# Moving the last loaded piece of a row-sum kernel to byte 64 of its buffer, with new bounds for the last two rows' pieces

## The chip, the cores and the metric

The kernel runs on one core of one Trainium2 chip. The metric is the device time of one execution in microseconds (us). A profiled execution has in addition a span, from its first to its last recorded instruction, some 1.35 us shorter than the time.

## The reference

```python
batch, seq, dim = 32, 512, 1024          # x: float32
relu_x = np.maximum(x, 0)
return np.sum(relu_x, axis=-1).astype(np.float32)
```

16,384 rows of 1024 floats are clipped at zero and summed: 67.1 MB in, 65 KB out.

## The kernel before

Each of the 128 partitions takes 128 rows. SyncE issues all loads: large chunks of 16 rows, then 8, 4 and 2 rows, and at last two rows cut by columns into four pieces. VectorE and ScalarE clip and sum. The last two rows matter here. Seen as one run of 2048 columns, they are cut so that the last transfer, the seam, holds the end of the first row and the head of the second in one small buffer of its own. Beside the seam's columns stand the partial sums of the other pieces, so that one instruction per row finishes both.

```python
CUT = 912
HEAD = 256
    ...
    w = D - CUT
    seam = nc.alloc_sbuf_tensor("seam", [P, 2 + w + HEAD + 2], fp32)
    ...
    first, second, third = [(0, CUT), (D + D // 2, 2 * D), (D + HEAD, D + D // 2)]
    for k, (lo, hi) in enumerate((first, second, third)):
        sp.dma_start(out=flat[:, lo:hi], in_=rows[:, lo:hi]).then_inc(...)
    sp.dma_start(out=seam[:, 2 : 2 + w + HEAD], in_=rows[:, CUT : D + HEAD]).then_inc(s_seam, 16)
    ...
    # first: half on each engine; second: ScalarE; third: VectorE
    act.wait_ge(s_seam, 16 + 2)
    act.wait_ge(s_half, 2)
    on_act(seam[:, 0:k], res[:, J - 2 : J - 1]).then_inc(s_last, 1)      # row 1: k = 2 + w
    dve.wait_ge(s_seam, 16 + 2)
    on_dve(seam[:, k : k + HEAD + 2], res[:, J - 1 : J]).then_inc(s_last, 1)   # row 2
```

The wait on `s_seam` counts 16 from the seam's transfer, one from ScalarE when the second piece is summed, and one from VectorE for the third. I call the moment at which it is full the **release**, and that at which a transfer's 16 counts are full its **landing**.

Of the kernel before, what the change touches and what calls it, by code (L numbers as in the profile page):

```python
# [3 lines left out]
P = 128  # L4
D = 1024
# [4 lines left out]
ACT_STEPS = [[16], [7, 9], [7, 9], [7, 9], [4, 5, 7], [3, 4, 5]]  # L10
DVE_STEPS = [[4, 5, 7], [7, 4, 5], [7, 4, 5], [7, 4, 5], [4, 5, 7], [3, 4, 5]]
TAIL = [8, 4, 2]
CUT = 912
HEAD = 256


def bass_relu_sum_kernel(
# [14 lines left out]
    fp32 = mybir.dt.float32  # L32
# [5 lines left out]
    J = B * S // P  # L38
# [11 lines left out]

    buf = nc.alloc_sbuf_tensor("buf", [P, NB, BIG, D], fp32)
    w = D - CUT
    seam = nc.alloc_sbuf_tensor("seam", [P, 2 + w + HEAD + 2], fp32)
    res = nc.alloc_sbuf_tensor("res", [P, J], fp32)
    turned = nc.alloc_sbuf_tensor("turned", [P, 32], fp32)

# [6 lines left out]
    s_half = nc.alloc_semaphore("s_half")  # L63
    s_seam = nc.alloc_semaphore("s_seam")
    s_last = nc.alloc_semaphore("s_last")
# [4 lines left out]
    sp, act, dve = nc.sync, nc.scalar, nc.vector  # L70
# [14 lines left out]
    for c in range(NBIG + 1):  # L85
        if c >= NB:
            sp.wait_ge(s_dve, done[c - NB])
        if c < NBIG:
            i = 0
            for g, j, n in CHUNKS[c]:  # L90
                sp.dma_start(  # L91
                    out=buf[:, c % NB, i : i + n, :], in_=xv[g][:, j : j + n, :]
# [14 lines left out]

    rows = xv[-1].rearrange("p j d -> p (j d)")[:, r * D : (r + 2) * D]
    flat = buf[:, tb, r : r + 2, :].rearrange("p j d -> p (j d)")
    first, second, third = [(0, CUT), (D + D // 2, 2 * D), (D + HEAD, D + D // 2)]  # L110
    for k, (lo, hi) in enumerate((first, second, third)):
        sp.dma_start(out=flat[:, lo:hi], in_=rows[:, lo:hi]).then_inc(  # L112
            s_in[NBIG + len(TAIL) + k], 16
        )
    sp.dma_start(out=seam[:, 2 : 2 + w + HEAD], in_=rows[:, CUT : D + HEAD]).then_inc(s_seam, 16)
    sp.wait_ge(s_turn, 1)
    sp.dma_start(
        out=of[0:P].rearrange("(k q) -> k q", q=32), in_=turned[0:P:32, 0:32]
# [7 lines left out]
    def on_act(t, acc):  # L126
        return act.activation(t, t, AF.Relu, accum_out=acc)  # L127

    def on_dve(t, acc):
        return dve.tensor_scalar(  # L130
            out=t, in0=t, scalar1=0.0, scalar2=None, op0=ALU.max, op1=ALU.add, accum_out=acc
        )
# [4 lines left out]
    k = 0  # L137
    for c in range(NTWO):
# [17 lines left out]
        for n in DVE_STEPS[c]:  # L156
            if ready[r + n - 1] > seen:
# [3 lines left out]
                out=res[:, c * BIG + r : c * BIG + r + n],  # L161
                in_=buf[:, c % NB, r : r + n, :],
# [24 lines left out]
    lo, hi = first  # L187
    act.wait_ge(s_in[-3], 16)
    dve.wait_ge(s_in[-3], 16)
    on_act(flat[:, lo : CUT // 2], seam[:, 0:1]).then_inc(s_half, 1)  # L190
    on_dve(flat[:, CUT // 2 : hi], seam[:, 1:2]).then_inc(s_half, 1)
    k = 2 + w
    lo, hi = second
    act.wait_ge(s_in[-2], 16)
    on_act(flat[:, lo:hi], seam[:, k + HEAD : k + HEAD + 1]).then_inc(s_seam, 1)
    lo, hi = third
    dve.wait_ge(s_in[-1], 16)
    on_dve(flat[:, lo:hi], seam[:, k + HEAD + 1 : k + HEAD + 2]).then_inc(s_seam, 1)
    act.wait_ge(s_seam, 16 + 2)
    act.wait_ge(s_half, 2)  # L200
    on_act(seam[:, 0:k], res[:, J - 2 : J - 1]).then_inc(s_last, 1)
    dve.wait_ge(s_seam, 16 + 2)
    on_dve(seam[:, k : k + HEAD + 2], res[:, J - 1 : J]).then_inc(s_last, 1)

# [33 lines left out]
```

## Time and profile before

| | before |
|---|---|
| time, median of 3 runs | 160.86 us (160.75 to 160.93) |
| span | 159.4 us |
| VectorE, ScalarE busy | 76%, 64% |
| load queue: time of its packets, as a share of the span of 16 DMA engines | 98.1% |
| HBM read and written over the span | 421 GB/s |
| release to issue of the last store | 0.48 us |

The chain of waits is to be read from its end: the last store, the two seam instructions, what released them. Where several events release one wait, the chain names one of them, so others that came within a few ns of it don't appear. Those are in the trace's records of semaphore updates, which I use beside the chain and which decide the order. A **packet** is one record of one DMA engine; each of the last four pieces is 128 packets, one for each partition, 8 on each engine.

### The profile page before, as it was taken

What the parts mean: (1) busy time and instruction counts of PE and PEld (TensorE: products, weight loads), DVE (VectorE), ACT (ScalarE), POOL (GpSimd) and SP (SyncE); (2) the same over time, 40 slices, a digit from 0 to 9 for tenths busy, and PEclk for the clock granted to TensorE, in tenths of its full rate; (3) what the DMA queues carried; (4) which work ended last, traced back from release to release, by engine and by line L of the source; (5) the groups of instructions that cost most, each with busy time, mean ns of one, the idle gap of its engine ahead of it and who ended that gap; (6) DMA issues with size and microseconds to landing.
All of it is one profiled execution on the core that took longest, in us unless ns stands there. A gap on an engine that the chain in (4) does not pass through costs nothing.

```text
span 159.4 us, 150 instructions
## 1 busy us (share of the span) xinstructions
DVE 120.6 (76%) x59; ACT 101.5 (64%) x54; POOL 0.2 (0%) x4
## 2 busy tenths in 40 slices
DVE  0000000009999999999999999999999999898995
ACT  3000059980799708996099941999329980496975
POOL 0000000000000000000000000000000000000000
DMA  9997996996996997989979969969969979798994
GB/s 378 493 401 339 493 526 263 526 526 263 526 493 296 526 444 345 526 378 411 526 312 477 526 263 526 526 263 526 526 263 526 444 345 526 321 469 374 417 400 142
DMA packets 2457, 67.18 MB, mean 421 GB/s; under 512 B 536, under 2 KB 792, under 8 KB 1176
## 3 DMA queue, kind: packets, MB, share of 16 engines
q1 hardware_dynamic: 2456, 67.18, 98.1%
q14 instruction: 1, 0.01, 0.0%
HBM read 67.11 MB, written 0.07 MB: 421 GB/s over the span
## 4 chain that ended last, share of the span: by engine, by line
DVE 55%; DMA 34%; ACT 9%; SPq 2%; issue 0%
DVE res L160 54%; DMA buf<-in_x_dram 34%; ACT buf L145 9%; SPq L101 1%; SPq L112 1%; DVE buf L130 0%; DVE seam L130 0%; SPq L91 0%; DVE turned L169 0%
## 5 line engine op out<-in xcount | busy, mean ns | idle before, releaser
L160 DVE TENSOR_REDUCE res<-buf 128x4 f32<-128x4096 f32 (+3 forms) x18 | 99.4, 5596 | 35.5 <-ACT buf L145 35.5
L145 ACT ACTIVATE buf<-buf 128x7168 f32<-128x7168 f32 (+5 forms) x13 | 80.4, 6233 | 46.1 <-DMA buf<-in_x_dram 46.1
L127 ACT ACTIVATE buf<-buf 128x1024 f32<-128x1024 f32 (+2 forms) x19 | 19.0, 999 | 8.9 <-DMA buf<-in_x_dram 8.9
L130 DVE TENSOR_SCALAR_CACHE_REDUCE buf<-buf 128x1024 f32<-128x1024 f32 (+2 forms) x19 | 20.7, 1143 | 1.7 <-DMA buf<-in_x_dram 1.6
L127 ACT ACTIVATION_READ_ACCUMULATOR buf<-buf 128x1 f32 x19 | 3.6, 188 | 0.0
L145 ACT ACT_TABLE_LOAD x1 | 1.3, 1283 | 1.3 <-PEq L223 1.3
L130 DVE DVE_READ_ACCUMULATOR buf<-buf 128x1 f32 x19 | 1.6, 84 | 0.0
L130 DVE TENSOR_SCALAR_CACHE_REDUCE seam<-seam 128x258 f32<-128x258 f32 x1 | 0.4, 421 | 0.0
L127 ACT ACTIVATE seam<-seam 128x114 f32<-128x114 f32 x1 | 0.3, 300 | 0.1
L169 DVE STREAM_TRANSPOSE turned<-res 128x32 f32<-128x32 f32 x1 | 0.2, 211 | 0.0
L127 ACT ACTIVATION_READ_ACCUMULATOR seam<-seam 128x1 f32 x1 | 0.2, 186 | 0.0
L223 POOL MEMSET const-bfloat16-1.0<- 128x1 bf16 x1 | 0.1, 101 | 0.0
L223 POOL MEMSET const-uint8-127<- 128x1 uint8 x1 | 0.1, 101 | 0.0
L223 POOL MEMSET const-float32-0.0<- 128x1 f32 x1 | 0.1, 98 | 0.2 <-issue 0.2
L223 POOL MEMSET const-float32-1.0<- 128x1 f32 x1 | 0.1, 98 | 0.0
L130 DVE DVE_READ_ACCUMULATOR seam<-seam 128x1 f32 x1 | 0.1, 82 | 0.0
## 6 DMA issues: line engine op xcount, KB each, us to landing
buf<-in_x_dram SPq DMA_DIRECT2D x1, 7680.0 KB, 21.1
buf<-in_x_dram SPq DMA_DIRECT2D x1, 4096.0 KB, 25.3
buf<-in_x_dram SPq DMA_DIRECT2D x1, 2048.0 KB, 29.9
buf<-in_x_dram SPq DMA_DIRECT2D x1, 1024.0 KB, 31.9
buf<-in_x_dram SPq DMA_DIRECT2D x1, 512.0 KB, 3.3
buf<-in_x_dram SPq DMA_DIRECT2D x1, 456.0 KB, 32.5
buf<-in_x_dram SPq DMA_DIRECT2D x1, 256.0 KB, 32.7
seam<-in_x_dram SPq DMA_DIRECT2D x1, 184.0 KB, 32.6
```

The costliest lines, as they stand in the source:

```text
L101: sp.dma_start(out=buf[:, tb, r : r + n, :], in_=xv[-1][:, r : r + n, :]).then_inc(s_in[NBIG + i], 16)
L112: sp.dma_start(out=flat[:, lo:hi], in_=rows[:, lo:hi]).then_inc(s_in[NBIG + len(TAIL) + k], 16)
L127: return act.activation(t, t, AF.Relu, accum_out=acc)
L130: return dve.tensor_scalar(out=t, in0=t, scalar1=0.0, scalar2=None, op0=ALU.max, op1=ALU.add, accum_out=acc)
L145: act.activation(t, t, AF.Relu).then_inc(s_act, 1)
L160: dve.tensor_reduce(out=res[:, c * BIG + r : c * BIG + r + n], in_=buf[:, c % NB, r : r + n, :], axis=X, op=ALU.add,).then_inc(s_dve, 1)
L169: dve.transpose(out=turned[:, :], in_=res[:, 0:32]).then_inc(s_turn, 1)
L223: nc = _bacc.Bacc("TRN2", target_bir_lowering=False, num_devices=1)
```

## The change

The intent: the seam's columns start 64 bytes into their buffer instead of 8, with the two partial sums of the first row just ahead of them. The bounds of the pieces move so that the seam also starts at a multiple of 256 bytes in memory, and the work is dealt anew between the engines.

```diff
-CUT = 912
-HEAD = 256
+CUT = 896
+HEAD = 240
+MID = 464
@@
+    z = 16
-    seam = nc.alloc_sbuf_tensor("seam", [P, 2 + w + HEAD + 2], fp32)
+    seam = nc.alloc_sbuf_tensor("seam", [P, z + w + HEAD + 2], fp32)
@@
-    first, second, third = [(0, CUT), (D + D // 2, 2 * D), (D + HEAD, D + D // 2)]
+    first, second, third = [(0, CUT), (D + MID, 2 * D), (D + HEAD, D + MID)]
@@
-    sp.dma_start(out=seam[:, 2 : 2 + w + HEAD], in_=rows[:, CUT : D + HEAD])...
+    sp.dma_start(out=seam[:, z : z + w + HEAD], in_=rows[:, CUT : D + HEAD])...
@@
-    on_act(flat[:, lo : CUT // 2], seam[:, 0:1])...
-    on_dve(flat[:, CUT // 2 : hi], seam[:, 1:2])...
-    k = 2 + w
+    on_act(flat[:, lo : CUT // 2], seam[:, z - 2 : z - 1])...
+    on_dve(flat[:, CUT // 2 : hi], seam[:, z - 1 : z])...
+    k = z + w
@@
-    on_act(seam[:, 0:k], res[:, J - 2 : J - 1])...
+    on_act(seam[:, z - 2 : k], res[:, J - 2 : J - 1])...
```

In columns: first piece 912 to 896, second 512 to 560, third 256 to 224, seam 368 before and after.

More of the change, by code (lines that the diff above doesn't have):

```diff
@@ L114, in bass_relu_sum_kernel @@
         )
-    sp.dma_start(out=seam[:, 2 : 2 + w + HEAD], in_=rows[:, CUT : D + HEAD]).then_inc(s_seam, 16)
+    sp.dma_start(out=seam[:, z : z + w + HEAD], in_=rows[:, CUT : D + HEAD]).then_inc(s_seam, 16)
     sp.wait_ge(s_turn, 1)
@@ L189, in bass_relu_sum_kernel @@
     dve.wait_ge(s_in[-3], 16)
-    on_act(flat[:, lo : CUT // 2], seam[:, 0:1]).then_inc(s_half, 1)
-    on_dve(flat[:, CUT // 2 : hi], seam[:, 1:2]).then_inc(s_half, 1)
-    k = 2 + w
+    on_act(flat[:, lo : CUT // 2], seam[:, z - 2 : z - 1]).then_inc(s_half, 1)
+    on_dve(flat[:, CUT // 2 : hi], seam[:, z - 1 : z]).then_inc(s_half, 1)
+    k = z + w
     lo, hi = second
@@ L200, in bass_relu_sum_kernel @@
     act.wait_ge(s_half, 2)
-    on_act(seam[:, 0:k], res[:, J - 2 : J - 1]).then_inc(s_last, 1)
+    on_act(seam[:, z - 2 : k], res[:, J - 2 : J - 1]).then_inc(s_last, 1)
     dve.wait_ge(s_seam, 16 + 2)
```

## The prediction

> **What bounds the kernel now.** I read the page first, for the load of the DMA engines, then the chain of waits in order of time, then the timeline of the last microseconds, then the groups by shape. The page:
>
> ```profile
> span 159.4 us, 150 instructions
> ...
> DMA  9997996996996997989979969969969979798994
> ...
> q1 hardware_dynamic: 2456, 67.18, 98.1%
> ```
>
> The one load queue keeps the 16 DMA engines busy 98.1% of the span; VectorE (76%) and ScalarE (64%) have slack. The kernel is a 67 MB load with a short tail, and the bytes are the same after the change. So only the tail can move. The end of the chain in order of time (start, length, what):
>
> ```profile
> 124.39 32.60 DMA buf<-in_x_dram
> 156.99 0.02 issue
> 157.01 0.44 DVE buf L130 x2
> 157.45 0.02 issue
> 157.47 0.43 DVE seam L130 x2
> ```
>
> The third piece lands at 156.99, VectorE reduces it until 157.45, both engines then do their share of the seam piece, and the last store follows (issue to landing 1.4, so the span closes at 159.4). The timeline of the tail (start, length, engine):
>
> ```profile
> 155.96 0.58 ACT L127 ACTIVATE buf<-buf 128x456 f32<-128x456 f32 x1
> 156.65 0.63 ACT L127 ACTIVATE buf<-buf 128x512 f32<-128x512 f32 x1
> 157.01 0.42 DVE L130 TENSOR_SCALAR_CACHE_REDUCE buf<-buf 128x256 f32<-128x256 f32 x1 [0.40 <-DMA buf<-in_x_dram]
> 157.19 0.19 ACT L127 ACTIVATION_READ_ACCUMULATOR buf<-buf 128x1 f32 x1
> 157.36 0.08 DVE L130 DVE_READ_ACCUMULATOR buf<-buf 128x1 f32 x1
> 157.47 0.30 ACT L127 ACTIVATE seam<-seam 128x114 f32<-128x114 f32 x1
> ```
>
> And the issues with their landing times:
>
> ```profile
> buf<-in_x_dram SPq DMA_DIRECT2D x1, 256.0 KB, 32.7
> seam<-in_x_dram SPq DMA_DIRECT2D x1, 184.0 KB, 32.6
> buf<-in_x_dram SPq DMA_DIRECT2D x1, 128.0 KB, 32.6
> ```
>
> Three arrivals release the seam's arithmetic: VectorE with the third piece (157.36 + 0.08 = 157.44, its semaphore at 157.451 in the semaphore records), the seam's own landing (issued 124.87, + 32.6; 157.438 in the records), and ScalarE with the second piece (157.19 + 0.19 = 157.38). They are 13 ns and 70 ns apart. That tie is the core of what follows: **no one of the three can be worth more than its lead over the next.**
>
> [...] the seam's last packet ends at 156.967 and its semaphore fills at 157.438, 0.47 later; this doesn't depend on where the piece lands, I take it.
> [...] Pieces of 3648, 2048 and 1024 bytes take 142, 84 and 46 ns at the median with little scatter (for 1024: 46 to 51). The line through 1024 and 3648 (0.0366 ns per byte, 8.5 ns fixed) gives 62.4 ns for 1472 bytes. The seam's 128 packets take 62 at the least (52 of them), 66 at the median, 67.5 at the mean, up to 82: the one piece at byte 8 is the one with a wide scatter.
>
> **The change part by part.**
> *Seam aligned, same size.* Destination at byte 64, and its source at 896 x 4 = 3584 = 14 x 256, also aligned. 128 packets over 16 engines are 8 an engine; each loses 67.5 - 62.4 = 5 ns, so 40 ns, and perhaps 60 in the engines that end last, whose packets are the slow ones. The seam lands at about 157.39.
> *Third piece, 256 to 224 columns.* First, second and third together hold 912 + 512 + 256 = 1680 columns before and 896 + 560 + 224 = 1680 after, so the third lands when it did, 156.99. VectorE's instruction gets shorter. The groups by shape (the last columns: busy us, mean ns | idle):
>
> ```profile
> L130 DVE TENSOR_SCALAR_CACHE_REDUCE buf<-buf 128x1024 f32<-128x1024 f32 x17 | 19.8, 1217 | 1.3 <-DMA buf<-in_x_dram 1.2
> L127 ACT ACTIVATE buf<-buf 128x1024 f32<-128x1024 f32 x17 | 17.7, 1045 | 8.9 <-DMA buf<-in_x_dram 8.9
> L127 ACT ACTIVATE buf<-buf 128x512 f32<-128x512 f32 x1 | 0.6, 630 | 0.0
> L130 DVE TENSOR_SCALAR_CACHE_REDUCE buf<-buf 128x256 f32<-128x256 f32 x1 | 0.4, 420 | 0.4 <-DMA buf<-in_x_dram 0.4
> ```
>
> VectorE: (1217 - 420) / 768 = 1.04 ns per column, so 32 columns are 33 ns, and VectorE's arrival moves from 157.451 to 157.418. ScalarE: (1045 - 630) / 512 = 0.81 ns per column.
> *First piece, 912 to 896.* Its halves go from 456 to 448 columns, and it lands 64 B x 8 packets x 0.037 = 19 ns earlier: off the path, since ScalarE waits for the second piece next.
> *Second piece, 512 to 560.* First and second together grow by 32 columns = 128 B: 128 x 8 x 0.037 = 38 ns later, so it lands at 156.626 + 0.038 = 156.664. ScalarE could start at 156.648 before (just free, 22 ns after the landing); now it starts at 156.664 + 0.022 = 156.686. Its instruction grows by 48 x 0.81 = 39 ns. Its arrival was 157.380; it becomes 157.380 + 0.038 + 0.039 = **157.457**.
> *The seam's arithmetic.* VectorE 258 to 242 columns, 16 x 1.04 = 17 ns less; it is the later one now (its semaphore at 157.915, ScalarE's at 157.873), so 17 ns on the path. ScalarE 114 to 130, 16 x 0.81 = 13 ns more, to 157.886 against VectorE's 157.898 at an unmoved release: still the earlier by 12 ns.
> *Sum.* Release max(157.39 seam, 157.418 VectorE, 157.457 ScalarE) = 157.457, against 157.451: +6. Then -17. Net **-11 ns**, in 160.86 us. Instruction counts and the order on each engine are unchanged[...].
>
> **Rivals.**
> *ScalarE is not delayed.* If the second piece's landing does not follow its bytes [...], ScalarE starts at 156.648, arrives at 157.419, ties with VectorE, and the release is 32 earlier: -32 - 17 = -49 ns, 160.81. For it: the steps between landings vary (0.37 for the 1024-byte piece against 0.48 for the seam at the mean). Against: those pieces' landings keep the order and roughly the spacing of their bytes.
> *Misaligned sources eat it.* The second piece now starts 64 B and the third 192 B above a 256 B boundary. [...] Against: the seam's source starts 64 B above a boundary today, yet 52 of its packets keep to the line of the aligned ones.
> *The seam's alignment is worth far more.* If landing at byte 8 cost the whole queue something [...], the pieces before it would also come earlier. The 3648, 2048 and 1024 packets sit on one line, so I see no room above 0.1 us.
> *Verdict-size effects.* For 2% the change must move 3.2 us, more than the whole tail from the third landing to the end (159.4 - 157.0 = 2.4). Nothing in it reaches that.
>
> **Range and chances.** The mean of the three ways, weighted to the first two, is -0.01 to -0.03: 160.84. The spread of the three runs of before is 0.18, larger than all three outcomes together; the session of another measurement may shift by as much. So 160.60 to 161.05. Faster by over 2%: 0.005; slower: 0.005; within: 0.99.
>
> **What would show it.** The seam's packets at a median near 62 ns with little scatter; the third landing unmoved at 156.99 (beside the same issue times); ScalarE's 560-column instruction near 669 ns and starting some 40 ns later; VectorE's 224 and 242 columns near 387 and 404 ns; the seam's arithmetic released by ScalarE, where the chain of waits now shows VectorE's third piece. Wrong if the seam's packets keep their scatter (alignment is then not its cause), if packets of the third piece rise above the line (8.5 + 0.0366 x 896 = 41 ns), or if the time moves by more than 0.25 us, which would mean that something before the tail changed.

The sum of the forecast: +6 ns at the release and 17 ns less after it, so -11 ns, or 160.85. The three ways together, weighted to the first two, came to -10 to -30 ns, hence 160.84. The way summed above (-11 ns) and "ScalarE is not delayed" (-49 ns, 160.81) keep their terms. The third, "Misaligned sources eat it", was weighed as a loss. That aligning the seam would pay was my estimate from the packets alone, 67.5 ns at the mean against 62.4 by the line.

## The result

| | before | after |
|---|---|---|
| time, median of 6 runs | 160.90 us (160.75 to 161.02) | 160.87 us (160.81 to 160.98) |
| ratio | | 1.000 (95% interval 0.9987 to 1.0013) |

A ratio is the mean time of one kernel's fast runs over that of the other's of the same rounds, so it isn't quite the ratio of the medians quoted. The profile page of the changed kernel:

```profile
span 159.5 us, 150 instructions
...
q1 hardware_dynamic: 2456, 67.18, 98.1%
```

The load is what it was. The end of its chain of waits in order of time (start, length, what):

```profile
123.97 32.82 DMA buf<-in_x_dram
156.79 0.02 issue
156.81 0.03 ACT buf L130
156.84 0.55 issue
157.39 0.20 ACT buf L130
157.58 0.02 issue
157.61 0.41 DVE seam L133 x2
```

The releaser has changed hands. Before, the chain ran through the third piece and VectorE. Now it runs through the second piece, landing at 156.79, and ScalarE's instruction on it. (The "issue" of 0.55 is the body of that instruction, whose two records the chain splits.) The timeline of the same stretch:

```profile
156.81 0.67 ACT L130 ACTIVATE buf<-buf 128x560 f32<-128x560 f32 x1
157.11 0.39 DVE L133 TENSOR_SCALAR_CACHE_REDUCE buf<-buf 128x224 f32<-128x224 f32 x1 [0.42 <-DMA buf<-in_x_dram]
157.39 0.19 ACT L130 ACTIVATION_READ_ACCUMULATOR buf<-buf 128x1 f32 x1
157.42 0.08 DVE L133 DVE_READ_ACCUMULATOR buf<-buf 128x1 f32 x1
157.61 0.31 ACT L130 ACTIVATE seam<-seam 128x130 f32<-128x130 f32 x1
```

VectorE is through with the third piece at 157.42 + 0.08 = 157.50, ScalarE with the second at 157.39 + 0.19 = 157.58, and the seam's instructions start at 157.61. The issues, with the time from issue to landing last:

```profile
buf<-in_x_dram SPq DMA_DIRECT2D x1, 280.0 KB, 32.8
seam<-in_x_dram SPq DMA_DIRECT2D x1, 184.0 KB, 32.6
```

The second piece took 32.7 before and 32.8 now; the seam has its 32.6 again. In the records:

| us from the span's start | before | after |
|---|---|---|
| the two-row piece ahead of these four has landed | 154.814 | 154.902 |
| seam has landed | 157.438 | 157.534 |
| VectorE's third piece counted | 157.451 | 157.516 |
| ScalarE's second piece counted | 157.380 | 157.584 |
| release to issue of the last store | 0.481 | 0.465 |
| span | 159.394 | 159.510 |

The whole queue ran 0.088 later in the profiled run of after, before any changed piece was due. From the two-row piece to the release it took 2.637 before and 2.682 after, 45 ns more, and from there to the store 16 ns less. 88 + 45 - 16 = 117 ns; the rest of the last store took 1 ns less, which makes the 116 ns by which the two spans differ. Only 29 ns of it lie in what was changed.

### The profile page after: what moved, and what is told of

Read it like the earlier page. It is cut to its first block, busy times and chain, and to the rows that moved or that the text cites. A ratio compares the mean times of both kernels' runs of the same rounds, so it can differ in the third digit from the quotient of the medians.

```text
span 159.5 us, 150 instructions
## 1 busy us (share of the span) xinstructions
DVE 120.6 (76%) x59; ACT 101.6 (64%) x54; POOL 0.2 (0%) x4
## 3 DMA queue, kind: packets, MB, share of 16 engines
q1 hardware_dynamic: 2456, 67.18, 98.1%
## 4 chain that ended last, share of the span: by engine, by line
DVE 55%; DMA 34%; ACT 9%; SPq 1%; issue 1%
DVE res L163 54%; DMA buf<-in_x_dram 34%; ACT buf L148 9%; SPq L104 1%; SPq L115 0%; DVE seam L133 0%; SPq L94 0%; ACT buf L130 0%; DVE turned L172 0%
## 6 DMA issues: line engine op xcount, KB each, us to landing
buf<-in_x_dram SPq DMA_DIRECT2D x1, 280.0 KB, 32.8
seam<-in_x_dram SPq DMA_DIRECT2D x1, 184.0 KB, 32.6
```

## The experiments

Three theories came out of the traces. **Theory 1:** the byte at which a piece lands in the buffer costs time. **Theory 2:** the byte at which it starts in memory does. **Theory 3:** neither, and the scatter of the seam's packets comes from its place in the queue. Beside these stands the claim that a tie of three arrivals sets the end. Packet times below are means from the trace's packet records; "line" is 8.5 ns + 0.0366 ns per byte, drawn through the medians of the pieces of 1024 and 3648 bytes of the kernel before (46 and 142 ns; the means are 46.3 and 144.4).

### land64_only and bounds_only: one half of the change each

land64_only, against after:

```diff
-CUT = 896
-HEAD = 240
-MID = 464
+CUT = 912
+HEAD = 256
+MID = 512
```

> The seam lands at byte 64, the bounds of before stay (912, 256, second and third piece cut at 512), so its source still starts 64 B above a multiple of 256 B. Theory 1 (the byte at which it lands costs): the seam's 1472-byte packets go from a mean of 67.5 ns to about 62.5 with hardly any scatter, and the seam lands some 40 ns earlier against the first piece; VectorE's third piece, 13 ns behind it before, still sets the release, so the time is the same within 0.05 us. Theory 2 (the scatter comes from where the source starts): the packets keep a mean near 67 ns. Theory 3 (neither; it comes from the end of the queue): also near 67 ns, here and in the kernels with an aligned source.

bounds_only, against after:

```diff
-    z = 16
+    z = 2
```

> The bounds of after, with the seam at byte 8 as before, its source on a multiple of 256 B. Theory 1: seam packets near 67 ns, seam landing later than in after by about 40 ns, and the release still set by ScalarE with the 560-column piece, so the time is that of after within 0.05 us. Theory 2: seam packets near 62 ns to 64.7, as in after. Both: packets of the second piece (source 64 B above a multiple of 256 B) at a mean near 94 ns with the scatter of after, above the 90.5 of the line.

### all_aligned and after_again

all_aligned, against after:

```diff
-HEAD = 240
-MID = 464
+HEAD = 256
+MID = 512
```

> CUT 896, HEAD 256, MID 512: every piece starts at a multiple of 256 B in the source and of 64 B in the destination; the seam grows to 384 columns (1536 B). Theory 2: all four pieces on the line (0.0366 ns per byte + 8.5), 140, 84, 46 and 64.7 ns, with little scatter; the third piece lands 19 ns earlier against the first chunk of the tail than before, VectorE releases the seam some 19 ns earlier than before, and the time is 160.85, the same within 0.1. Theory 3: the seam's packets still scatter, mean 3 ns or more above the line.

after_again is the changed kernel, unedited.

> The changed kernel once more, to see how far its trace repeats. If the tie of the three arrivals is read rightly, ScalarE's 560-column piece sets the release again, and packets of the second piece are again at a mean near 94 ns, of the seam near 64.7; differences between landings within 20 ns of those of the first trace. If they differ by 50 ns or more, one trace can't tell which part of the tail gained or lost.

What these four gave, all on one chip, where the kernel before, run beside them, had a median of 160.88 (160.82 to 161.10). "Seam late by" is its landing after that of the two-row piece, both averaged over the 16 DMA engines.

| | lands at byte, seam's source | seam's packets, ns (line) | second piece's packets (line) | seam late by, us | releaser | two-row piece to release, us | time, us | ratio |
|---|---|---|---|---|---|---|---|---|
| before (first trace) | 8, 64 B off | 67.5 (62.4) | 84.6 (83.5) | 2.665 | VectorE | 2.637 | 160.88 | 1 |
| land64_only | 64, 64 B off | 66.0 (62.4) | 84.1 (83.5) | 2.687 | VectorE and seam | 2.665 | 161.07 | 1.0008 |
| bounds_only | 8, aligned | 64.3 (62.4) | 93.8 (90.5) | 2.674 | ScalarE | 2.635 | 160.99 | 1.0002 |
| all_aligned | 64, aligned | 72.1 (64.7) | 85.1 (83.5) | 2.681 | seam and VectorE | 2.656 | 160.93 | 1.0004 |
| after (first trace) | 64, aligned | 64.7 (62.4) | 94.3 (90.5) | 2.679 | ScalarE | 2.682 | | |
| after_again | 64, aligned | 64.7 (62.4) | 93.8 (90.5) | 2.677 | ScalarE | 2.680 | 161.06 | 1.0013 |

Every interval includes 1. Theory 1 asked for a seam 40 ns earlier in land64_only; it came 22 ns later. It asked for one 40 ns later in bounds_only than in after; it came 5 ns earlier. Theory 2 fails at all_aligned, where everything is aligned and the seam's packets lie furthest above the line of the table, 7.4 ns. (The third piece landed no earlier there either, 2.187 us after the two-row piece against 2.188 before, averaged over the engines. But with 16 columns fewer ahead of it the count of bytes asked for 19 ns whatever the theory, so that speaks against sums this fine and not against theory 2.) The column "seam late by" is the plainest: 22 ns between the extremes, whatever lands where.

The last columns show the other half: the bounds, not the landing byte, decide who releases. With HEAD 256 and MID 512 VectorE's third piece and the seam's landing come last, within 15 ns of each other (before: 157.451 and 157.438; land64_only: 157.557 and 157.564; all_aligned: 157.467 and 157.482; the chain names VectorE in all three, the semaphore records give the order). With HEAD 240 and MID 464 it is ScalarE's second piece, by 25 to 50 ns. The stretch to the release is not so firm. after and after_again agree within 2 ns, but bounds_only, with the same bounds, was 45 to 47 ns shorter, so one trace can't tell which of these versions is better.

Much of the difference between times lies outside this stretch. The profiled span of land64_only is 0.311 us longer than that of before. Of this, 0.085 came before the two-row piece had landed, 0.028 before the release and 0.196 after the issue of the last store, where 1.658 remained against 1.462.

### split512 and split512_byte8: the landing byte, over the whole load

One small piece is a poor gauge. So the six chunks of 16 rows were loaded as column halves: 1536 packets of 2 KiB on each DMA engine, for an effect of a few ns a packet to add up. split512, against before (the waits on a chunk then count 32):

```diff
-                sp.dma_start(
-                    out=buf[:, c % NB, i : i + n, :], in_=xv[g][:, j : j + n, :]
-                ).then_inc(s_in[c], 16)
+                for lo, hi in ((0, 512), (512, D)) if c else ((0, D),):
+                    sp.dma_start(
+                        out=buf[:, c % NB, i : i + n, lo:hi], in_=xv[g][:, j : j + n, lo:hi]
+                    ).then_inc(s_in[c], 16)
```

> The kernel before, with the six chunks of 16 rows loaded as two column halves of 512 (2048-byte packets; both halves start at a multiple of 256 B, landing at a multiple of 64 B). It is the control of the other splits, with 1536 such packets on each of the 16 DMA engines. At 84 to 86 ns a packet against 2418 ns per 65536 bytes (75.6 per 2048), it takes about 13 to 16 us longer than before: 174 to 177 us. Packets at 84 ns with little scatter.

split512_byte8 has that and a buffer that starts 8 bytes on:

```diff
-    buf = nc.alloc_sbuf_tensor("buf", [P, NB, BIG, D], fp32)
+    room = nc.alloc_sbuf_tensor("buf", [P, NB * BIG * D + 16], fp32)
+    buf = room[:, 2 : 2 + NB * BIG * D].rearrange("p (b r d) -> p b r d", b=NB, r=BIG)
```

> As the split at 512, but everything lands 8 bytes further on, [...] as the seam did before. Theory 1 (the byte at which a piece lands costs 5 ns a packet): 1536 packets an engine add about 7.7 us to the split at 512, packets near 89 ns. If the cost were in proportion to bytes (67.5/62.4, 8%), about 12 us. Theories 2 and 3: within 0.5 us of the split at 512.

From the pages, first split512, then split512_byte8 (span; busy us; the load queue's packets, MB, share of 16 engines; the reads):

```profile
span 173.7 us, 156 instructions
...
DVE 121.5 (70%) x59; ACT 101.5 (58%) x54; POOL 0.2 (0%) x4
...
q1 hardware_dynamic: 26360, 67.18, 101.9%
...
HBM read 67.11 MB, written 0.07 MB: 387 GB/s over the span
```

```profile
span 173.6 us, 156 instructions
...
DVE 121.5 (70%) x59; ACT 101.5 (58%) x54; POOL 0.2 (0%) x4
...
q1 hardware_dynamic: 26360, 67.18, 102.0%
...
HBM read 67.11 MB, written 0.07 MB: 387 GB/s over the span
```

The control's time came in as expected, 174.93 us (174.91 to 175.05), ratio 1.0876 to before (160.80 beside it; in before's trace, with 50 of the 67 MB in 64-KiB packets, the load ran at 421 GB/s over the span, here at 387); its packets did not, 88.8 ns where 84 were expected. The shifted one took 175.01 (174.95 to 175.01), 0.08 more where theory 1 asked for 7.7. Packets of 2048 bytes averaged 88.8 and 88.9 ns. The engines, whose operands are shifted too, are as busy as before. So the landing byte costs nothing that these runs can see, and theory 1 is out. (Both kernels stand 5.4 ns above the line; a cost that hides under whatever makes that excess would not show.)

That excess is mostly no delay. From 40 to 140 us of split512 the 16 engines moved 387 GB/s at a packet share of 105%: at that rate 2048 bytes leave an engine every 2048 x 16 / 387 = 84.7 ns, while a packet's record is 88.8 ns long. The records of neighbouring packets overlap, so a longer record need not mean that the queue lost that time.

### split528 and split368: where a piece starts in memory

The same edit as split512 with 528 or 368 in place of 512.

> Split at 528: 2112-byte packets from an aligned source, 1984-byte packets whose source starts 64 B above a multiple of 256 B; both land at multiples of 64 B. Theory 2 (where the source starts costs): the 1984-byte packets lie 3 ns or more above their line (81.1 ns), so 768 an engine add 2.3 us or more to the time of the split at 512. Theory 3: both on the line, time within 0.5 us of the split at 512.

> Split at 368: 1472-byte packets from an aligned source (the seam's size after the change) and 2624-byte packets whose source starts 192 B above a multiple of 256 B; both land at multiples of 64 B. Theory 2: 1472-byte packets at 62 ns without scatter, 2624-byte ones above their line (104.5 ns). Theory 3: where a mean over the line shows up here in the 1472-byte ones too, it is not the start of source or destination; 62 ns on all of them would leave the end of the queue as the cause of the seam's scatter.

| split | packets of the first part: mean ns, over the line | of the second part | both | time, us |
|---|---|---|---|---|
| 512 | 2048 B, aligned: 88.8, +5.4 | 2048 B, aligned: 88.8, +5.4 | 177.7 | 174.93 |
| 528 | 2112 B, aligned: 88.3, +2.5 | 1984 B, 64 B off: 88.6, +7.5 | 176.9 | 174.88 |
| 368 | 1472 B, aligned: 69.1, +6.7 | 2624 B, 192 B off: 107.5, +3.0 | 176.6 | 174.99 |

The three times lie within 0.11 us of each other. Where theory 2 asked for 2.3 us more at 528, it took 0.05 less. The packet that starts off 256 B is the further above the line at 528, but the nearer to it at 368, and the aligned 1472-byte packets show the very excess that I had put down to misalignment. A packet's own time shifts from one part to the other while the pair takes nearly, and the load quite, the same. Theory 2 is out as a cost of time.

### seam_then_third: the place in the queue

Against before, the seam's transfer is issued ahead of the third piece's:

```diff
     for k, (lo, hi) in enumerate((first, second, third)):
+        if k == 2:
+            sp.dma_start(out=seam[:, 2 : 2 + w + HEAD], in_=rows[:, CUT : D + HEAD]).then_inc(
+                s_seam, 16
+            )
         sp.dma_start(out=flat[:, lo:hi], in_=rows[:, lo:hi]).then_inc(
             s_in[NBIG + len(TAIL) + k], 16
         )
-    sp.dma_start(out=seam[:, 2 : 2 + w + HEAD], in_=rows[:, CUT : D + HEAD]).then_inc(s_seam, 16)
```

> The kernel before, with the seam's transfer issued ahead of the third piece's. Does the scatter of packet times belong to the last piece in the queue or to the size? If to the last place: the seam's 1472-byte packets at 62 ns, the 1024-byte ones with scatter above 46. If to the size (or what its rows hold): 1472 at a mean of 67 again, 1024 at 46. The third piece now lands last, at about 157.44, and VectorE's 0.42 + 0.08 come after it, so the release and the end move by 0.45 to 0.5: about 161.3.

The seam's packets, still landing at byte 8 from a source 64 B off, fell from 67.5 to 62.9 ns: on the line, with nothing about their addresses or size changed. So in this one trace the excess went with the place and not with the piece. But the 1024-byte packets, now last, only rose from 46.3 to 46.8, so "the last place scatters" isn't the rule either.

All traces with the seam last sort by what stands ahead of it. Behind pieces of 2048 and 1024 bytes its packets lie 3.6 to 7.6 ns above the line (before, land64_only, all_aligned and the four split kernels, whose tail is that of before). Behind pieces of other sizes it is 1.0 to 2.7 (bounds_only, after, after_again and the two kernels below). The first group's seam starts off 256 B as well, in all but all_aligned, so that one kernel, with a slightly larger seam, is what separates the order from the source here. This sorting was found afterwards and no run was made to test it.

The time was 161.39 (161.26 to 161.51), ratio 1.0023 (1.0006 to 1.0040), where 161.3 was expected: the third piece now lands last, at 157.47, and VectorE's work on it comes after. From the two-row piece to the release it took 3.098 us against 2.637, 0.46 more where 0.45 to 0.5 was expected.

### second_768 and second_256: pulling the tie apart

Against after, one number each; the second piece gets 768 or 256 columns and the third 16 or 528:

```diff
-MID = 464
+MID = 256        # second_768; second_256 has 768
```

> The changed kernel with MID 256: the second piece (ScalarE) has 768 columns, the third (VectorE) 16. If ScalarE's arrival sets the release in the changed kernel, the second piece lands 208 columns x 4 B x 8 packets x 0.0366 ns = 0.24 later and ScalarE takes 208 x 0.81 ns = 0.17 more: the release and the end move by 0.41, to 161.28 where the changed kernel has 160.87. If the three arrivals don't set the end [...], the time stays within 0.1.

> The changed kernel with MID 768: second piece 256 columns, third 528 (VectorE). The third lands when it did, VectorE takes 304 x 1.04 ns = 0.32 more; it was 0.07 ahead of the release, so the end moves by 0.24 to about 161.11, with VectorE as the releaser in the chain of waits. If the tie does not matter: within 0.1 of 160.87.

The ends of the two chains of waits, first second_768:

```profile
157.00 0.02 ACT buf L130
157.03 0.72 issue
157.75 0.20 ACT buf L130
157.95 0.02 issue
157.97 0.41 DVE seam L133 x2
```

Then second_256:

```profile
157.12 0.02 issue
157.14 0.72 DVE buf L133 x2
157.87 0.02 issue
157.89 0.41 DVE seam L133 x2
```

In one ScalarE releases, in the other VectorE. From the two-row piece to the release it took 3.082 and 2.901, against 2.682 in after: +0.40 where 0.41 was expected, and +0.22 where 0.24 was. The times were 161.25 (161.23 to 161.31) and 161.15 (161.04 to 161.33), against the 161.28 and 161.11 expected; the kernel before, run on the same chip beside them and rather scattered there, had 160.94 (160.79 to 161.45). The ratio of second_768 is clear of 1, 1.0016 (1.0003 to 1.0028); that of second_256, 1.0009, is not. The reading of the tie holds, and its sums are good to some 20 ns when they are pushed well out of the tie.

## Why the prediction was right

The time, 160.87, lies 0.03 from the 160.84 foretold. That closeness is partly luck: the six runs of after alone spread over 0.17, and both outcomes whose sums stand in the prediction (160.81 and 160.85) lie within that. Not all of the steps were right.

- **The load bounds the kernel; only the tail can move.** Right: 98.1% and 421 GB/s in both, and no tail version above moved the time by more than half a microsecond.
- **No arrival is worth more than its lead over the next.** Right, and it is why a wrong step did no harm: a seam 40 ns earlier could have given nothing, since another arrival was later still, VectorE's by 13 ns before and ScalarE's by 50 ns after.
- **The seam aligned, 40 to 60 ns.** Wrong. It was worth nothing: measured from the two-row piece, the seam landed at 2.624 before and 2.632 after (the full counts of the table of the result), and the means of 49 thousand packets of split512 and split512_byte8 differ by less than 0.1 ns. The sign that was asked for half came, without its cause: the median fell from 66 to 62 and the mean to 64.7, with packets up to 79 ns still, but so they did in bounds_only, at byte 8 (62 and 64.3). Two inferences failed. The first was from "the one piece at byte 8 is the one with a wide scatter". The scatter was real, but that piece differed from the others in its place in the queue and in its source as well, and all_aligned and split368 have it without misalignment. Nor was it the only one: four of the 128 packets of 3648 bytes in the same trace took 171 to 241 ns. The second was from "each loses 5 ns" to "so 40 ns": where records overlap, as they do by 5% in split512 (and the packet share was 109% from 156.0 to 156.5 us of before, where the seam begins), a packet's excess need not be time lost. In after the mean fell by 2.8 ns, which would be 22 ns on 8 packets, and the seam landed 14 ns later (2.679 against 2.665, averaged over the engines). One assumption held, by one trace each: from the end of the seam's last packet to its landing it took 0.471 us before, at byte 8, and 0.469 after, at byte 64.
- **Third piece unmoved, VectorE 33 ns shorter.** Right: measured from the two-row piece it landed at 2.174 before and 2.185 after, and the instruction took 385 ns, 35 less.
- **Second piece 38 ns later, ScalarE 39 ns longer.** ScalarE's instruction took the 669 ns foretold. The landing was mis-sized: averaged over the engines and measured from the two-row piece, it came 1.821 us after it before, and 1.883, 1.888 and 1.883 in after, after_again and bounds_only, so 62 to 67 ns later. Its packets at 94 ns instead of the line's 90.5 are of the size of the rest, 3.5 ns x 8 packets = 28, but before's stood 1.1 above their line too, and records overlap, so this sum is not shown to be the cause.
- **Release +6, then -17.** The new releaser was right, the second number too (0.481 to 0.465). The first measured +45 in the trace of after, 43 in after_again and -2 in bounds_only, so 6 is not refuted, only finer than one trace can show. The term that was off is the landing of the second piece: by the last of its 16 engines, which is what ScalarE waits for, it came 77, 75 and 29 ns later instead of 38. 6 + 77 - 38 = 45, 6 + 75 - 38 = 43 and 6 + 29 - 38 = -3 are the three measured values within 1 ns.
- **The rivals.** "ScalarE is not delayed" fell in the trace: the second piece landed 62 ns later. "Misaligned sources eat it" has no size to check, but its reason was not seen: the third piece, 192 B off, kept to 42.0 ns against a line of 41.3 and landed 11 ns later, and split528 took no longer than split512 (174.88 against 174.93 us).

**What stays open** is why packets of some pieces take a few ns more than the line: the seam's (1.0 to 7.6 above it where it is last, by kernel) and the 560-column second piece's (3.3 to 3.8). Landing byte, source byte and size alone are each spoken against by a run above; in the one trace of seam_then_third the excess went with the order in the queue (67.5 to 62.9 ns), which of its features is not shown. It costs the total nothing that shows: the seam lands 2.665 to 2.687 us after the two-row piece in every kernel in which it is last and of which the table speaks. None of the versions tried beats the kernel before clear of the noise.

## What to carry to other kernels

When several arrivals release one wait within a few tens of ns, work out the lead of each over the next before valuing any of them; a gain on one is worth at most that lead, and rebalancing can just move the last place to another engine, as here from VectorE (157.451 in before) to ScalarE (157.584 in after). A scatter seen in one piece of 128 packets is a hint and not a price: apply the suspected condition to the whole load, where a few ns a packet would add up to microseconds (5 ns on 1536 packets an engine, 7.7 us; split512_byte8 took 0.08 more), before building on it. A packet's record is not its price either where records overlap: check it against the rate (88.8 ns against 84.7 in split512). Below the scatter between runs (here 0.2 to 0.7 us, by session) compare landings and releases within a trace, and take a second trace to learn how far these repeat.
